# Reordering the first loads, the casts of later inputs and the stores of w1 in a seven-product MLP kernel

## The chip, the cores and the metric

The kernel runs on one core of one Trainium2 chip. The metric is device time of one execution in microseconds (us). In the profile PE is TensorE (matmul), PEld its weight loads, DVE is VectorE, ACT is ScalarE, POOL is GpSimd and SP is SyncE; a `q` after the name (SPq) means the engine's sequencer issuing DMA. PEclk is the share of full clock that the throttle granted to TensorE.

## The reference

```python
# x [8, 1024, 1024], w1 [1024, 4096], w2 [4096, 1024], all float32
h = x @ w1
h = 0.5 * h * (1 + np.tanh(np.sqrt(2 / np.pi) * (h + 0.044715 * h ** 3)))
return (h @ w2).astype(np.float32)
```

## The kernel before

The 8192 tokens go through in eight superblocks of 1024. Each matrix product is split into 2x2 blocks and done with seven block products in place of eight (Strassen's scheme, one level), which takes 448 matmuls of 128x128 by 128x512 for a layer of a superblock. Products 2 and 5 use a raw block of the weight; the other five use a sum or difference of two blocks. These seven "operands" in fp16 are made once, in superblock 0, stored to DRAM (14.7 MB for each weight) and loaded from there in every later superblock. The second layer of superblock 0 is done plainly, with 512 matmuls, while the operands of w2 are being made.

Three parts matter. The first is how superblock 0 makes w1: 512-byte runs of w1 in, a cast on ScalarE, five sums on VectorE, and three stores at once from the POOL queue.

```python
w1v = w1.rearrange("(k p) (b c n) -> b c p k n", p=P, b=2, n=P)    # n = 128 floats = 512 bytes

def make_w1(c):                      # for each of 16 column blocks, in superblock 0
    raw = {}
    for b in range(2):
        st = gcp.tile([P, 2 * KH, P], F32, name="gc")              # 3 buffers
        nc.sync.dma_start(out=st, in_=w1v[b, c])                   # SP queue
        r = rawp.tile([P, 2, KH * P], DT, name="raw")              # 5 buffers
        nc.scalar.copy(out=r..., in_=st...)                        # ACT cast to fp16
        ...
    ops = w_operands([v[:, j] for j in range(5)], raw)             # DVE: five sums
    nc.gpsimd.dma_start(out=w1_d[c][:, 0:5, :], in_=v)             # POOL queue
    for j, m in enumerate(PLAIN):
        nc.gpsimd.dma_start(out=w1_d[c][:, 5 + j, :], in_=ops[m])  # releases raw
    ...
```

The second is how x of a later superblock comes in: eight casting DMAs (fp32 to fp16, DRAM to DRAM) from the POOL queue into rows of 128 elements (256 bytes), then eight transposing DMAs from the SP queue.

```python
def x_later(s):
    xr = x2[s * SB:(s + 1) * SB, :].rearrange("t (k c) -> k t c", c=P)
    xb = xdram.tile([2 * KH, SB, P], DT, name="xb")
    xT = xtp.tile([P, 2 * KH, SB], DT, name="xT")
    for k in range(2 * KH):
        nc.gpsimd.dma_start(out=xb[k], in_=xr[k])
    for k in range(2 * KH):
        nc.sync.dma_start(out=xT[:, k, :], in_=xb[k], transpose=True)
    return xT
```

The third is the loop. The text calls the casts of the next superblock after the first layer of this one. The scheduler that turns the text into instruction streams did not keep that order: in the trace of the kernel before these casts, which have no input but x itself, were issued from 1.3 us on.

```python
xT = x_first()                       # superblock 0: x transposed by PE
for sb in range(NSB):
    xs = x_sums(xT)
    g = matmul1(xs, make_w1 if sb == 0 else load_w1)
    if sb + 1 < NSB:
        xT = x_later(sb + 1)
    (matmul2_first if sb == 0 else matmul2)(sb, g)
```

In `matmul2_first` the fp32 rows of w2 are loaded on the SP queue, cast on ScalarE, used, summed on VectorE and stored from the POOL queue.

Of the kernel before, what the change touches and what calls it, by code (L numbers as in the profile page):

```python
# [8 lines left out]
F32 = mybir.dt.float32  # L9
# [39 lines left out]
PLAIN = (2, 5)  # L49


@with_exitstack
def kernel(
# [21 lines left out]
    WP = 8  # L75

    xtp = ctx.enter_context(tc.tile_pool(name="xtp", bufs=2))
    xsp = ctx.enter_context(tc.tile_pool(name="xsp", bufs=1))
    gp = ctx.enter_context(tc.tile_pool(name="gp", bufs=1))
    gcp = ctx.enter_context(tc.tile_pool(name="gcp", bufs=3))  # L80
    wp = ctx.enter_context(tc.tile_pool(name="wp", bufs=6))
    rawp = ctx.enter_context(tc.tile_pool(name="rawp", bufs=5))
# [6 lines left out]
    w1v = w1.rearrange("(k p) (b c n) -> b c p k n", p=P, b=2, n=P)  # L89
    w2v = w2.rearrange("(a c p) (b o) -> b c p a o", a=2, p=P, b=2)  # L90

    w1_d = [dram.tile([P, 7, KH * P], DT, name=f"w1_d{c}") for c in range(NI)]
    w2_d = [dram.tile([P, 7, WP, OH], DT, name=f"w2_d{h}") for h in range(NI // WP)]
# [7 lines left out]
    def wtile():  # L101
        return wp.tile([P, WP * OH], DT, name="w")
# [3 lines left out]
    def w_operands(sums, raw):  # L106

        ops = {}
        for j, m in enumerate(SUMS):
            u, op, v = B_TERMS[m]  # L110
            nc.vector.tensor_tensor(out=sums[j], in0=raw[u], in1=raw[v], op=op)  # L111
            ops[m] = sums[j]
        for m in PLAIN:
            ops[m] = raw[B_TERMS[m][0]]
        return ops

    def make_w1(c):
        raw = {}
        for b in range(2):
            st = gcp.tile([P, 2 * KH, P], F32, name="gc")  # L120
            nc.sync.dma_start(out=st, in_=w1v[b, c])
            r = rawp.tile([P, 2, KH * P], DT, name="raw")
            nc.scalar.copy(out=r.rearrange("p a f -> p (a f)"), in_=st.rearrange("p k n -> p (k n)"))  # L123
            for a in range(2):
                raw[f"{a + 1}{b + 1}"] = r[:, a]
        t = wtile()
        v = t[:, : 5 * KH * P].rearrange("p (m f) -> p m f", m=5)
        ops = w_operands([v[:, j] for j in range(5)], raw)
        nc.gpsimd.dma_start(out=w1_d[c][:, 0:5, :], in_=v)
        for j, m in enumerate(PLAIN):  # L130
            nc.gpsimd.dma_start(out=w1_d[c][:, 5 + j, :], in_=ops[m])  # L131
        return {m: o.rearrange("p (k n) -> p k n", n=P) for m, o in ops.items()}

    def load_w1(c):
        t = wtile()
        nc.sync.dma_start(out=t[:, : 7 * KH * P], in_=w1_d[c].rearrange("p m f -> p (m f)"))
        v = t[:, : 7 * KH * P].rearrange("p (m k n) -> p m k n", m=7, n=P)
        return {m: v[:, j] for j, m in enumerate(SUMS + PLAIN)}

    def load_w2(m):  # L140
        j = (SUMS + PLAIN).index(m)
        pieces = []
        for h in range(NI // WP):
            t = wtile()
            nc.sync.dma_start(
                out=t, in_=w2_d[h][:, j].rearrange("p c o -> p (c o)")
            )
            pieces.append(t.rearrange("p (c o) -> p c o", o=OH))
        return pieces
# [3 lines left out]
    def x_sums(xT):  # L153
        blocks = {
            f"{a + 1}{k + 1}": xT[:, k * KH:(k + 1) * KH, a * HT:(a + 1) * HT]
            for a in range(2) for k in range(2)
        }
        ops = {3: blocks["11"], 4: blocks["22"]}
        for m in (5, 1, 2, 7, 6):
            u, v = A_TERMS[m]  # L160
            s = xsp.tile([P, KH, HT], DT, name=f"xs{m}")
            nc.vector.tensor_tensor(out=s, in0=blocks[u], in1=blocks[v], op=SUB)
            ops[m] = s
        return ops

    def x_first():
        identity = consts.tile([P, P], F32, name="identity")
        make_identity(nc, identity)
        xT = xtp.tile([P, 2 * KH, SB], DT, name="xT")
        for s in range(SB // P):  # L170
            xn = tp.tile([P, HT], F32, name="tmp")
            xm = tp.tile([P, HT], F32, name="tmp")
            for k, t in enumerate((xn, xm)):
                nc.sync.dma_start(out=t, in_=x2[s * P:(s + 1) * P, k * HT:(k + 1) * HT])
                ps = psum()
                for j in range(KH):
                    nc.tensor.matmul(
                        ps[:, j * P:(j + 1) * P],
                        lhsT=t[:, j * P:(j + 1) * P],
                        rhs=identity,  # L180
                        is_transpose=True,
                        start=(j == 0),
                        stop=(j == KH - 1),
                    )
                eng = nc.vector.tensor_copy if k == 0 else nc.scalar.copy
                eng(  # L186
                    out=xT[:, k * KH:(k + 1) * KH, s * P:(s + 1) * P],
                    in_=ps.rearrange("p (j t) -> p j t", t=P),
                )
        return xT  # L190

    def x_later(s):
        xr = x2[s * SB:(s + 1) * SB, :].rearrange("t (k c) -> k t c", c=P)
        xb = xdram.tile([2 * KH, SB, P], DT, name="xb")
        xT = xtp.tile([P, 2 * KH, SB], DT, name="xT")
        for k in range(2 * KH):
            nc.gpsimd.dma_start(out=xb[k], in_=xr[k])  # L197
        for k in range(2 * KH):
            nc.sync.dma_start(out=xT[:, k, :], in_=xb[k], transpose=True)
        return xT  # L200

    def tt(out, in0, in1, op):
        nc.vector.tensor_tensor(out=out, in0=in0, in1=in1, op=op)  # L203
# [3 lines left out]
    def matmul1(xs, get_w1):  # L207
        g = {b: gp.tile([P, NI, HT], GT, name=f"g{b}") for b in ("11", "12", "21", "22")}

        def product(bank, w, m, first, last):  # L210
            for k in range(KH):
                nc.tensor.matmul(  # L212
                    bank,
                    lhsT=w[m][:, k, :],
                    rhs=xs[m][:, k, :],
                    start=(first and k == 0),
                    stop=(k == KH - 1),
                    skip_group_check=not first,
                )
# [11 lines left out]

        for c in range(NI):
            w = get_w1(c)
# [23 lines left out]
            late = (c, w, qb, s2)  # L257
        finish(*late)
        return g
# [3 lines left out]
    def store(sb, b, q, src):  # L263
        r0 = sb * SB + (int(b[0]) - 1) * HT + q * P
        o0 = (int(b[1]) - 1) * OH
        nc.gpsimd.dma_start(out=out2[r0:r0 + P, o0:o0 + OH], in_=src)  # L266

    def matmul2_first(sb, g):
# [3 lines left out]
        keep = []  # L272
        for b in range(2):
# [3 lines left out]
            def mm(i, c, w):  # L277
                for a in range(2):
# [3 lines left out]
                        rhs=w[:, a, :],  # L282
# [4 lines left out]
            for c in range(NI):  # L287
                st = gcp.tile([P, 2, OH], F32, name="gc")
                nc.sync.dma_start(out=st, in_=w2v[b, c])
                if b == 0:  # L290
                    if c % 4 == 0:
                        keep.append(wtile().rearrange("p (c a o) -> p c a o", a=2, o=OH))
                    w = keep[-1][:, c % 4]
                else:
                    w = rawp.tile([P, 2, OH], DT, name="raw")
                nc.scalar.copy(out=w, in_=st)  # L296
                ready.append(w)
                if c < NI - TAIL:
                    for i in range(2 * NQ):
                        mm(i, c, w)  # L300
                if b == 1:
                    w0 = keep[c // 4][:, c % 4]
                    raw = {"11": w0[:, 0], "21": w0[:, 1], "12": w[:, 0], "22": w[:, 1]}
                    t = wtile()
                    v = t[:, : 5 * OH].rearrange("p (m o) -> p m o", m=5)
                    ops = w_operands([v[:, j] for j in range(5)], raw)
                    d = w2_d[c // WP]
                    nc.gpsimd.dma_start(out=d[:, 0:5, c % WP, :], in_=v)  # L308
                    for j, m in enumerate(PLAIN):
                        nc.gpsimd.dma_start(out=d[:, 5 + j, c % WP, :], in_=ops[m])  # L310
            for i in range(2 * NQ):
# [7 lines left out]
                store(sb, f"{i // NQ + 1}{b + 1}", i % NQ, o)  # L319

    def matmul2(sb, g):
        def product(m, banks, first):
            pieces = load_w2(m)
            u, v = A_TERMS[m]
            for q in range(NQ):
# [8 lines left out]
                for c in range(NI):  # L334
# [3 lines left out]
                        rhs=pieces[c // WP][:, c % WP, :],  # L338
# [30 lines left out]
        for q, ps in product(7, rb, False):  # L369
            c11 = temp()  # L370
            tt(c11, u[q], ps, ADD)
            store(sb, "11", q, c11)

    xT = x_first()
    for sb in range(NSB):
        xs = x_sums(xT)
        g = matmul1(xs, make_w1 if sb == 0 else load_w1)
        if sb + 1 < NSB:
            xT = x_later(sb + 1)
        (matmul2_first if sb == 0 else matmul2)(sb, g)  # L380
# [30 lines left out]
```

## Time and profile before

| | before |
|---|---|
| median of 4 runs | 1723.96 us (1721.97 to 1725.25) |
| first product starts | 25.5 us |
| first layer of superblock 0, 448 matmuls | 222 us, granted clock 0.76 |
| second layer of superblock 0, 512 matmuls | about 111 us |
| each later superblock, 896 matmuls | 193.4 us |

The first fence is the window view of the kernel before, for four stretches: the start, the first layer, the second layer, and superblock 1. The columns are the stretch, its length, the busy time of each engine with the number of its instructions, the granted clock, the mean share of the 16 DMA engines that was in use (the recorded times of packets are added up, and the sum passes 1 here, with 1.16 and 1.33), and the rate.

```profile
core 0: us, PE busy (x) PEld busy (x) DVE busy (x) ACT busy (x) POOL busy (x), PEclk, DMA share, GB/s
0.00:25.50 25.50, 15.18 (x64) 11.04 (x65) 7.55 (x11) 6.72 (x10) 9.06 (x17) 0.87 1.16 248
25.50:247.50 222.00, 126.66 (x454) 50.20 (x454) 85.60 (x167) 87.01 (x124) 66.79 (x105) 0.76 1.33 245
247.50:358.60 111.10, 111.10 (x511) 50.21 (x510) 36.42 (x91) 25.40 (x29) 33.04 (x51) 0.99 0.92 285
358.60:552.00 193.40, 193.21 (x897) 87.50 (x895) 95.94 (x125) 53.85 (x93) 8.68 (x16) 1.00 0.59 193
```

TensorE is busy all of superblock 1, and so it is in the six after that: 896 matmuls at 0.216 us are 193.4 us. That is the floor of these stages. The first layer of superblock 0 has half as many matmuls and needs 222 us in place of 97. In this stretch the DMA share is above 1 while the rate is only 245 GB/s: the DMA engines are busy and yet do not move much.

The next fence is the chain of waits on the page of the kernel before (the work that ended last, followed back to its releasers), by line. After it comes the view of the tile that the casts write.

```profile
DMA xb<-in_x_dram 9%; POOL out_dram L266 4%; DMA w_d_93<-w 1%; DMA out_dram<-tmp 1%; POOL w_d_103 L310 0%; POOL w_d_102 L310 0%; POOL w_d_102 L308 0%; POOL w_d_103 L308 0%; POOL xb L197 0%; POOLq L266 0%; POOL w_d_101 L131 0%; POOL w_d_100 
```

```profile
L197 POOL DMA_DIRECT2D xb<-in_x_dram x56: 751/758/895, 1.3 to 169.7; - x56
```

The casts in this chain are 9% of the span, about 155 us, and all 56 of them, for all seven later superblocks, were issued between 1.3 and 169.7 us, inside superblock 0. Their 57,344 packets (56 casts of 1024 rows) are three quarters of the 76,672 packets of queue q0.

Three more views show what the casts do to others. The first two are the timeline of POOL, with the two stores of raw blocks of the first column block, and a line of the timeline of ACT. Each line of a timeline has the start, the length, the engine, the line of the source, the operation, and in brackets the idle time before it with what ended it.

```profile
33.56 0.58 POOL L131 DMA_DIRECT2D w_d_86<-raw  x1 [3.24 <-DMA xb<-in_x_dram]
...
57.44 0.57 POOL L131 DMA_DIRECT2D w_d_86<-raw  x1 [0.97 <-DMA xb<-in_x_dram]
```

```profile
54.17 1.05 ACT L123 CAST raw<-gc 128x1024 f16<-128x1024 f32 x1 [14.01 <-DMA w_d_86<-raw]
```

A line from the view of the tile that those stores write (times from issue to landing, in us):

```profile
DMA to landing us min/median/max: 4.4/4.5/20.5
```

On POOL, between the first of these stores (33.6 us) and the second (57.4 us) stand nine casts, and POOL paused before all but one of them for an earlier cast. The first store also needed 20.5 us from issue to landing, where 4.5 is the median; it shares its DMA queue with the casts, but that this is the reason is not shown. Until it landed, at about 54.1 us, it held its raw buffer, and the cast on ACT that needed the buffer had waited 14.0 us ("<-DMA w_d_86<-raw"). The next cast on ACT came at 69.7 us, after another 14.0 us.

The third is the timeline of the SP queue. The text `x2` at the end of a line is the number of instructions in it.

```profile
71.17 4.53 SPq L199 DMA_TRANSPOSE xT<-xb  x1
81.90 0.37 SPq L121 DMA_DIRECT2D gc<-in_w_dram  x1
82.33 9.28 SPq L199 DMA_TRANSPOSE xT<-xb  x2
...
92.28 14.65 SPq L199 DMA_TRANSPOSE xT<-xb  x2
...
107.66 9.42 SPq L199 DMA_TRANSPOSE xT<-xb  x1
...
117.80 12.83 SPq L199 DMA_TRANSPOSE xT<-xb  x2
130.72 79.15 SPq L121 DMA_DIRECT2D gc<-in_w_dram  x18
```

Transposes of x for superblock 1 stand in the same queue as the loads of w1 (L121). The queue did one thing at a time: none of its DMA records (346) overlaps the next. Five times between 71 and 131 us the queue stands at transposes: 4.53 + 9.28 + 14.65 + 9.42 + 12.83 = 50.7 us. No load was issued in that time.

### The profile page before, as it was taken

What the parts mean: (1) busy time and instruction counts of PE and PEld (TensorE: products, weight loads), DVE (VectorE), ACT (ScalarE), POOL (GpSimd) and SP (SyncE); (2) the same over time, 40 slices, a digit from 0 to 9 for tenths busy, and PEclk for the clock granted to TensorE, in tenths of its full rate; (3) what the DMA queues carried; (4) which work ended last, traced back from release to release, by engine and by line L of the source; (5) the groups of instructions that cost most, each with busy time, mean ns of one, the idle gap of its engine ahead of it and who ended that gap; (6) DMA issues with size and microseconds to landing.
All of it is one profiled execution on the core that took longest, in us unless ns stands there. A gap on an engine that the chain in (4) does not pass through costs nothing.

```text
span 1723.7 us, 18773 instructions
## 1 busy us (share of the span) xinstructions
PE 1606.4 (93%) x7296; PEld 724.8 (42%) x7296; DVE 801.8 (47%) x1136; ACT 495.8 (29%) x806; POOL 170.2 (10%) x286
## 2 busy tenths in 40 slices
PE   5246789999999999999999999999999999999997
PEld 3012334444444444444444444444444444444443
DVE  4123642445534555345534565345534565355433
ACT  3123661234310441034310441034310441034310
POOL 2333222310011000100011000100011000100011
PEclk8667899999999999999999999999999999999999
DMA  9999999874765447554755447554755444554451
GB/s 234 210 204 224 308 305 245 285 292 158 199 213 180 152 165 210 197 193 153 218 197 179 155 169 205 198 187 153 213 202 186 158 169 154 199 179 155 169 195 49
DMA packets 210425, 336.78 MB, mean 195 GB/s; under 512 B 125600, under 2 KB 158368, under 8 KB 197792
## 3 DMA queue, kind: packets, MB, share of 16 engines
q1 hardware_dynamic: 133664, 257.98, 49.8%
q0 software_dynamic: 76672, 77.61, 18.2%
q8 instruction: 57, 0.93, 0.2%
q14 instruction: 32, 0.26, 0.0%
HBM read 272.63 MB, written 77.59 MB: 203 GB/s over the span
## 4 chain that ended last, share of the span: by engine, by line
issue 82%; DMA 11%; POOL 6%; POOLq 0%
DMA xb<-in_x_dram 9%; POOL out_dram L266 4%; DMA w_d_93<-w 1%; DMA out_dram<-tmp 1%; POOL w_d_103 L310 0%; POOL w_d_102 L310 0%; POOL w_d_102 L308 0%; POOL w_d_103 L308 0%; POOL xb L197 0%; POOLq L266 0%; POOL w_d_101 L131 0%; POOL w_d_100 L131 0%; POOL w_d_99 L131 0%; POOL w_d_98 L131 0%; POOL w_d_97 L131 0%
## 5 line engine op out<-in xcount | busy, mean ns | idle before, releaser
L203 DVE TENSOR_TENSOR tmp<-tmp,ps 128x512 f32<-128x512 f32 x652 | 447.2, 687 | 699.6 <-PE ps L335 332.3
L212 PEld LDWEIGHTS <-w 128*128 128x128 f16 x3456 | 342.0, 99 | 502.3 <-issue 105.8
L335 PE MATMUL ps<-w,gc 128*128 128x512 f16 x2240 | 485.8, 379 | 0.0
L335 PEld LDWEIGHTS <-gc 128*128 128x128 bf16 x2240 | 219.3, 98 | 264.2
L212 PE MATMUL ps<-xT,w 128*128 128x512 f16 x1024 | 267.7, 384 | 0.7 <-ACT xT L186 0.7
L266 POOL DMA_DIRECT2D out_dram<-tmp x128 | 69.5, 543 | 1327.9 <-ACT tmp L355 951.8
L237 ACT COPY tmp<-ps 128x512 f32<-128x512 f32 x128 | 72.9, 569 | 251.6 <-PE ps L212 251.6
L203 DVE TENSOR_TENSOR tmp<-ps,tmp 128x512 f32<-128x512 f32 x128 | 88.4, 690 | 5.0 <-PE ps L212 0.7
L111 DVE TENSOR_TENSOR w<-raw 128x512 f16<-128x512 f16 x96 | 37.8, 420 | 69.2 <-ACT raw L123 69.2
L123 ACT CAST raw<-gc 128x1024 f16<-128x1024 f32 x32 | 33.4, 1043 | 121.0 <-DMA gc<-in_w_dram 62.9
L355 ACT COPY tmp<-ps 128x512 f32<-128x512 f32 x28 | 16.4, 586 | 177.3 <-PE ps L335 177.3
L212 PE MATMUL ps<-xs_246,w 128*128 128x512 f16 x64 | 21.0, 461 | 45.9 <-ACT g_249 L222 45.9
L197 POOL DMA_DIRECT2D xb<-in_x_dram x56 | 42.5, 761 | 80.5 <-DMA xb<-in_x_dram 76.7
L212 PE MATMUL ps<-xs_244,w 128*128 128x512 f16 x64 | 20.3, 448 | 31.9 <-DVE tmp L203 31.9
L361 ACT COPY tmp<-ps 128x512 f32<-128x512 f32 x28 | 16.4, 586 | 80.3 <-PE ps L335 54.0
L349 ACT COPY tmp<-ps 128x512 f32<-128x512 f32 x28 | 16.4, 586 | 74.4 <-PE ps L335 74.4
L212 PE MATMUL ps<-xs_242,raw 128*128 128x512 f16 x64 | 20.3, 449 | 15.4 <-ACT tmp L237 15.4
L212 PEld LDWEIGHTS <-raw 128*128 128x128 f16 x128 | 14.4, 113 | 39.5 <-issue 26.7
L111 DVE TENSOR_TENSOR w<-w,raw 128x512 f16<-128x512 f16 x48 | 18.6, 419 | 18.0 <-ACT raw L296 18.0
L296 ACT CAST raw<-gc 128x1024 f16<-128x1024 f32 x16 | 16.7, 1045 | 34.8 <-PE ps L279 24.5
L279 PE MATMUL ps<-w,g_249 128*128 128x512 f16 x64 | 25.0, 391 | 0.0
L279 PE MATMUL ps<-w,g_248 128*128 128x512 f16 x64 | 24.8, 387 | 0.0
(236 smaller groups left out, 1759.6 us busy)
## 6 DMA issues: line engine op xcount, KB each, us to landing
w<-w_d_102 SPq DMA_DIRECT2D x49, 1024.0 KB, 5.0
w<-w_d_103 SPq DMA_DIRECT2D x49, 1024.0 KB, 7.0
gc<-in_w_dram SPq DMA_DIRECT2D x64, 512.0 KB, 6.8
out_dram<-tmp POOLq DMA_DIRECT2D x128, 256.0 KB, 2.7
xb<-in_x_dram POOLq DMA_DIRECT2D x56, 256.0 KB, 16.1
w<-w_d_86 SPq DMA_DIRECT2D x7, 896.0 KB, 4.5
w<-w_d_87 SPq DMA_DIRECT2D x7, 896.0 KB, 6.1
w<-w_d_88 SPq DMA_DIRECT2D x7, 896.0 KB, 6.3
```

Of the source, the lines that this page charges most:

```text
L111: nc.vector.tensor_tensor(out=sums[j], in0=raw[u], in1=raw[v], op=op)
L123: nc.scalar.copy(out=r.rearrange("p a f -> p (a f)"), in_=st.rearrange("p k n -> p (k n)"))
L197: nc.gpsimd.dma_start(out=xb[k], in_=xr[k])
L203: nc.vector.tensor_tensor(out=out, in0=in0, in1=in1, op=op)
L212: nc.tensor.matmul(bank, lhsT=w[m][:, k, :], rhs=xs[m][:, k, :], start=(first and k == 0), stop=(k == KH - 1), skip_group_check=not first,)
L237: nc.scalar.copy(out=v, in_=pb)
L266: nc.gpsimd.dma_start(out=out2[r0:r0 + P, o0:o0 + OH], in_=src)
L279: nc.tensor.matmul(banks[i], lhsT=g[f"{i // NQ + 1}{a + 1}"][:, c, (i % NQ) * P:(i % NQ + 1) * P], rhs=w[:, a, :], start=(c == 0 and a == ...
L296: nc.scalar.copy(out=w, in_=st)
L335: nc.tensor.matmul(banks[q], lhsT=a[:, c, :], rhs=pieces[c // WP][:, c % WP, :], start=(first and c == 0), stop=(c == NI - 1), skip_group_ ...
L349: nc.scalar.copy(out=v[q], in_=ps)
L355: nc.scalar.copy(out=c21, in_=ps)
```

## The change

The change has several parts: first loads in one strict order with 2 KB runs; raw fp16 w1 to DRAM first, and its sums made and stored one superblock later; one pool of 26 buffers of 4 KB per partition ("units") in place of several pools. One more part is in the diff: the casts of x are 128 whole rows (2 KB of fp16 each) and are ordered behind another instruction, so that they can no longer be pulled to the start. The diff, cut to its core:

```diff
-    w1v = w1.rearrange("(k p) (b c n) -> b c p k n", p=P, b=2, n=P)
+    w1v = w1.rearrange("(k p) (b i) -> b p k i", p=P, b=2)
+    raw_d = [dram.tile([P, 4, KH * QW], DT, name=f"raw_d{q}") for q in range(NI // QC)]
+    up = ctx.enter_context(tc.tile_pool(name="up", bufs=26))
...
+    def load_in_order(out, in_, **kw):
+        return tc.keep_in_program_order(nc.sync.dma_start(out=out, in_=in_, **kw))
...
+    class MadeQuad:                 # a quarter of w1: 4 column blocks, 512 floats = 2 KB runs
+        def load(self):
+            for b, t in self.raw.items():
+                for k in range(0, KH, 2):
+                    cast_in(t[:, k:k + 2, :], w1v[..., self.q * QW:(self.q + 1) * QW],
+                            nc.scalar.copy if k else pool_copy)
+        def sum(self, m, sl=slice(None)):
+            make_sum(self.ops, m, self.raw, KH, QW, sl)
+            if not self.first:      # superblock 1, not 0
+                nc.gpsimd.dma_start(out=w1_d[self.q][:, m - 1, :], in_=flat(self.ops[m]))
+        def keep_raw(self):         # superblock 0: 2.1 MB for a quarter, not 3.7
+            for b, t in self.raw.items():
+                load_in_order(raw_d[self.q][:, BLOCKS.index(b), :], flat(t))
...
-        for k in range(2 * KH):
-            nc.gpsimd.dma_start(out=xb[k], in_=xr[k])
+    def x_cast(s, after):
+        xb = xdram.tile([SB, H], DT, name="xb")
+        with tc.issue_after(after.ins):
+            for q in range(0, SB, P):
+                nc.gpsimd.dma_start(out=xb[q:q + P, :], in_=x2[s * SB + q:s * SB + q + P, :])
+        return xb
...
+        if sb == 0:
+            xb = x_cast(1, pool_last[0])        # behind the last w1 cast on POOL
+            last, blocks = matmul2_first(sb, g, quad.keep_raw, xb)
+            continue
         if sb + 1 < NSB:
-            xT = x_later(sb + 1)
-        (matmul2_first if sb == 0 else matmul2)(sb, g)
+            blocks = x_transpose(x_cast(sb + 1, last), nc.sync.dma_start)
+        last = matmul2(sb, g)                   # last: this superblock's last output store
```

Superblock 1 loads the raw blocks, makes the sums again and stores all seven operands. The transposes for superblock 1 go to the end of the second layer of superblock 0.

## The prediction

> **What bounds it now.** From 358.0 to 1712.3 us TensorE never waits: the window table shows 193.40 us for each of the seven later superblocks (896 matmuls of 0.216 us), all busy. That part is at its floor. The loss lies in the first superblock. Its first product starts at 25.5 us (timeline), and the 448 matmuls of its first layer take 222 us (25.5 to 247.5) where 448 x 0.216 = 97 us would do, at a granted clock of 0.76. Its second layer (512 matmuls, to 358.0) is at its floor of 110.5 us. After the last matmul come 11.5 us.
>
> The 125 us are lost to DMA: from 25.5 to 175 us the share of the 16 engines is 1.47, at only 213 GB/s, and the chain of waits runs from 4.8 to 173 us almost wholly through the x casts. The view of the cast tile shows all 56 casts, for all seven later superblocks, issued between 1.3 and 169.7 us. They write 256-byte rows: 57,344 packets of about 41 ns, over 16 engines some 147 us of engine time (an estimate from the packet records). Beside them run w1 loads in 512-byte packets, stores of finished operands (14.7 MB), and transposes that hold up the w1 loads behind them on the SP queue. [...] without the casts, from 190 to 240 us, the rate is 317 GB/s.
>
> **What the change does.** The casts go behind the last POOL cast, later behind each superblock's last store, in 2 KB rows: out of the first layer. The finished w1 stores move to superblock 1. Left in the first layer: x 4.2 MB, w1 16.8 MB, 6.3 MB of raw stores. A quarter of w1 is 4.2 MB in 2 KB packets (101 ns each here: 13 us) plus a 2.1 MB store in 4 KB packets (160 ns: 5 us), 18 us against 24.2 us of matmul: TensorE should bind. VectorE comes near: per quarter 20 x 0.69 + 5 x 1.22 = 20 us, more in the first.
>
> Start: the x transposes (0.93 us per four) take some 19 us, then w1's first columns; first product about 21.5 us. First layer 97 [...] + 6 (waits for quarter 1 and VectorE) = 106, to 127.5 us. Second layer 110.5, to 238; its sums, stores and transposes fit within. For the boundary and superblock 1 (raw loads 8.4 MB, stores 14.7 MB) I allow 5. Then 7 x 193.4 = 1354 and 11.5: 238 + 5 + 1354 + 11.5 = 1608.
>
> **Predicted: 1608 us**, 8 in 10 between 1592 and 1640. Faster by over 2%: 0.96; within 2%: 0.03; slower: 0.01.
>
> **What would show it.** Right: first product near 21.5 us, second layer from near 128 us, no cast packets in the first 80 us, later superblocks still 193.4 us. Partly wrong: PE waits in the first quarters on VectorE sums or ScalarE/POOL casts; PE waits at superblock 1's start on transposes or on units held by unfinished stores.
>
> **What would make it wrong.** The 26 units are almost all in use (25 in superblock 1): a late store delays the next quarter's load, then TensorE. The strict queue can block on one full buffer. [...] a POOL cast of several us would starve the first quarters. Superblock 1's 33 MB in 97 us is near the most this trace shows (408 GB/s in 10 us). Each costs 10 to 40 us, not the gain.

Two statements on the hardware that no trace of this case shows are cut from this text, and in the sum of the first layer a term of 3 us, for which no trace is named. With the term that sum was 97 + 3 + 6 = 106 us; without it the terms left come to 103. The 1608 us still contain it (1605 without it).

## The result

The kernel after takes 1619.66 us, the median of four runs (1617.7 to 1620.44). The ratio to the kernel before is 0.9394, with a 95% interval of 0.9378 to 0.9411. Ratios here are the mean time of one kernel's fast runs over that of the other's of the same rounds, so they are not quite the ratio of the medians quoted.

The window view of the kernel after, with four stretches that have the same meaning as before:

```profile
0.00:26.70 26.70, 11.14 (x64) 10.15 (x64) 12.90 (x15) 7.62 (x12) 5.14 (x10) 0.82 0.75 245
26.70:139.70 113.00, 101.81 (x449) 44.73 (x450) 76.24 (x109) 74.36 (x113) 22.18 (x25) 0.95 0.91 308
139.70:249.00 109.30, 109.30 (x508) 49.59 (x507) 46.20 (x44) 20.77 (x25) 12.22 (x23) 1.00 1.00 349
249.00:442.60 193.60, 191.97 (x889) 86.73 (x888) 106.20 (x135) 53.91 (x93) 22.82 (x44) 1.00 0.66 225
```

The first layer fell from 222 to 113 us, at a clock of 0.95 in place of 0.76. The second layer and the later superblocks are as they were. The rate in the first layer rose from 245 to 308 GB/s at a lower share. The chain of waits and the view of the cast tile:

```profile
PE ps L267 33%; PE ps L439 30%; PE ps L375 3%; DMA gc<-in_w_dram 2%; DVE u L107 1%; POOL out_dram L355 1%; DMA u<-raw_d_82 1%; SPq L115 1%; DMA u<-raw_d_83 1%; DMA gc<-in_x_dram 1%; ACT u L137 1%; PE ps L225 0%; DMA xb<-in_x_dram 0%; DMA ou
```

```profile
L244 POOL DMA_DIRECT2D xb<-in_x_dram x56: 486/516/652, 88.0 to 1226.5; - x56
```

No cast comes before 88.0 us, and the chain is now mostly matmuls. What TensorE still waits for is small. These are the two longest in the view of PE's waits (what waited and for what; total us, number, longest):

```profile
PE ps L267 <- ACT tmp L324: 8.9, 1, 8.9
PE ps L267 <- DVE u L107: 8.2, 1, 8.2
```

Both lie in the first layer. The one of 8.2 us is at the first product, the one of 8.9 us at 101 us. The timeline shows the first of them:

```profile
19.34 9.13 DVE L107 TENSOR_TENSOR u<-u 128x2048 f16<-128x2048 f16 x10
...
26.73 5.47 PE L267 MATMUL ps<-u 128*128 128x512 f16 x15 [8.23 <-DVE u L107]
```

VectorE does ten operations in a row. The five differences of x come first among them, and the first sum of w1, which the first product needs, comes after. So the first product waited 8.23 us for VectorE. The second wait, from the same timeline:

```profile
106.19 1.04 ACT L137 CAST u<-gc 128x1024 f16<-128x1024 f32 x1 [9.04 <-DMA gc<-in_w_dram]
...
109.11 0.56 ACT L324 COPY tmp<-ps 128x512 f32<-128x512 f32 x1
...
109.73 3.63 PE L267 MATMUL ps<-u 128*128 128x512 f16 x9 [8.90 <-ACT tmp L324]
```

On ACT a cast of w2 stood before the gelu and the copy that TensorE needed. The SP queue issued four loads of w2 from 88.35 us on, this one among them, and the cast could not start before 106.19 us. It waited 9.04 us, and TensorE then 8.90 us for the copy at 109.11. Between 90 and 100 us the loads got only 24 GB/s, beside 152 GB/s written by the eight casts for superblock 1 (issued from 88.0 us) and 113 GB/s of raw stores (packet records). So the moved casts may themselves hold up this load; no run tests it.

The following table is taken from the order of the matmul records in each trace: start of the first product, then the time to the 449th matmul (first layer), to the end of the 512 plain ones (second layer), and through superblock 1. A few records can be missing, so the stages are good to about a microsecond. Superblocks 2 to 7 took 193.4 us each in every run. The ratio is to the kernel before (medians of 1722.8 to 1725.2 us). Kernels are compared only within the same rounds. All outputs are right.

| run | ratio (95%) | median us | first product | first layer | second layer | superblock 1 |
|---|---|---|---|---|---|---|
| before | 1 | 1724.0 | 25.5 | 220.3 | 112.2 | 193.7 |
| after | 0.9394 (0.9378 to 0.9411) | 1619.7 | 26.7 | 112.8 | 110.5 | 195.6 |
| b1_defer_casts | 0.9415 (0.9401 to 0.9429) | 1624.7 | 20.0 | 132.3 | 110.6 | 194.7 |
| b2_wide_casts | 0.9935 (0.9901 to 0.9968) | 1715.3 | 32.7 | 204.7 | 110.5 | 195.3 |
| a1_early_casts | 0.9678 (0.9661 to 0.9694) | 1670.0 | 51.8 | 140.9 | 110.5 | 195.0 |
| a2_store_w1_at_once | 0.9467 (0.9451 to 0.9483) | 1634.4 | 27.5 | 127.0 | 113.6 | 193.4 |
| a4_512B_w1_runs | 0.9458 (0.9442 to 0.9474) | 1628.6 | 25.5 | 122.7 | 110.5 | 196.5 |
| c1_defer_and_spread | 0.9408 (0.9394 to 0.9422) | 1620.2 | 19.0 | 115.8 | 111.8 | 205.5 |
| c2_defer_spread_wide | 0.9475 (0.9461 to 0.9489) | 1632.0 | 18.4 | 124.5 | 110.5 | 204.4 |
| c3_casts_behind_gelu | 0.9448 (0.9435 to 0.9461) | 1629.1 | 18.9 | 109.7 | 129.9 | 203.3 |
| a3_w2_casts_on_pool | 0.9395 (0.9381 to 0.9409) | 1618.5 | 26.3 | 112.5 | 113.1 | 193.8 |
| v1_w2_casts_behind_gelu | 0.9409 (0.9396 to 0.9422) | 1621.7 | 26.6 | 102.0 | 117.4 | 204.0 |
| v2_first_sum_first | 0.9378 (0.9365 to 0.9391) | 1615.9 | 19.3 | 107.9 | 110.5 | 206.0 |
| v3_first_stores_own_queue | 0.9357 (0.9339 to 0.9375) | 1614.4 | 19.8 | 107.5 | 121.5 | 196.5 |

From before to after the stages sum to +1.2 - 107.5 - 1.7 + 1.9 = -106.1 us, and the two profiled executions differ by 107.8 us (spans 1723.7 and 1615.9; the rest is after the last matmul). The timed medians differ by 104.3 us. The profiled execution of the kernel after was the fastest of its four.

### The profile page after: what moved, and what is told of

Same layout as the page of the kernel before. It is cut to its first block, busy times and chain, and to the rows that moved or that the text cites. A ratio compares the mean times of both kernels' runs of the same rounds, so it can differ in the third digit from the quotient of the medians.

```text
span 1615.9 us, 19003 instructions
## 1 busy us (share of the span) xinstructions
PE 1577.7 (98%) x7296; PEld 718.5 (44%) x7296; DVE 819.7 (51%) x1046; ACT 480.5 (30%) x794; POOL 135.0 (8%) x238
## 4 chain that ended last, share of the span: by engine, by line
PE 66%; issue 23%; DMA 5%; DVE 1%; POOL 1%; SPq 1%; ACT 1%; POOLq 0%; DVEq 0%; ACTq 0%
PE ps L267 33%; PE ps L439 30%; PE ps L375 3%; DMA gc<-in_w_dram 2%; DVE u L107 1%; POOL out_dram L355 1%; DMA u<-raw_d_82 1%; SPq L115 1%; DMA u<-raw_d_83 1%; DMA gc<-in_x_dram 1%; ACT u L137 1%; PE ps L225 0%; DMA xb<-in_x_dram 0%; DMA out_dram<-tmp 0%; SPq L152 0%
## 5 line engine op out<-in xcount | busy, mean ns | idle before, releaser
L267 PE MATMUL ps<-u 128*128 128x512 f16 x3584 | 780.3, 380 | 21.0 <-ACT tmp L324 8.9
L267 PEld LDWEIGHTS <-u 128*128 128x128 f16 x3584 | 351.3, 98 | 448.8 <-issue 21.4
L439 PE MATMUL ps<-u,gc 128*128 128x512 f16 x2240 | 485.8, 379 | 0.0
L107 DVE TENSOR_TENSOR u<-u 128x2048 f16<-128x2048 f16 (+2 forms) x110 | 123.2, 1151 | 58.1 <-ACT u L137 24.7
L324 ACT COPY tmp<-ps 128x512 f32<-128x512 f32 x128 | 72.9, 569 | 261.9 <-PE ps L267 261.8
L459 ACT COPY tmp<-ps 128x512 f32<-128x512 f32 x28 | 16.4, 587 | 177.3 <-PE ps L439 177.3
L137 ACT CAST u<-gc 128x1024 f16<-128x1024 f32 (+1 forms) x52 | 50.2, 978 | 46.0 <-DMA gc<-in_w_dram 45.9
L375 PE MATMUL ps<-u,g_220 128*128 128x512 f16 x128 | 48.5, 379 | 0.0
L375 PE MATMUL ps<-u,g_221 128*128 128x512 f16 x128 | 48.5, 379 | 0.0
L375 PE MATMUL ps<-u,g_222 128*128 128x512 f16 x128 | 48.5, 379 | 0.0
L375 PE MATMUL ps<-u,g_223 128*128 128x512 f16 x128 | 48.5, 379 | 0.0
L465 ACT COPY tmp<-ps 128x512 f32<-128x512 f32 x28 | 16.4, 586 | 80.3 <-PE ps L439 80.3
L453 ACT COPY tmp<-ps 128x512 f32<-128x512 f32 x28 | 16.4, 586 | 74.9 <-PE ps L439 74.9
L244 POOL DMA_DIRECT2D xb<-in_x_dram x56 | 27.6, 514 | 14.4 <-DMA out_dram<-tmp 10.4
L118 POOL CAST u<-gc 128x1024 f16<-128x1024 f32 (+1 forms) x20 | 22.6, 1131 | 64.1 <-DMA gc<-in_w_dram 54.5
L419 ACT COPY tmp<-ps 128x512 f32<-128x512 f32 x8 | 4.7, 585 | 64.7 <-PE ps L375 64.7
L375 PEld LDWEIGHTS <-g_221 128*128 128x128 bf16 x128 | 12.5, 98 | 15.1
L375 PEld LDWEIGHTS <-g_223 128*128 128x128 bf16 x128 | 12.5, 98 | 15.1
```

What stands on the lines that cost most here:

```text
L107: nc.vector.tensor_tensor(out=out, in0=in0, in1=in1, op=op)
L118: pool_last[0] = nc.gpsimd.tensor_copy(out=out, in_=in_)
L137: cast(out=dst, in_=st)
L244: nc.gpsimd.dma_start(out=xb[q:q + P, :], in_=x2[s * SB + q:s * SB + q + P, :])
L267: nc.tensor.matmul(bank, lhsT=ops[m][:, k, cs], rhs=xs[m][:, k, :], start=(first and k == 0), stop=(k == KH - 1), skip_group_check=not first,)
L324: nc.scalar.copy(out=v, in_=pb)
```

## The experiments

The theory to test: the early casts of x are what made the first layer slow, and moving them is what gained. The rivals: the wider runs of w1 and the later stores gained, or it was not where the casts stand but their small packets.

### One part alone, on the kernel before

**b1_defer_casts** is the kernel before with only the order changed: each superblock's casts are issued behind the last DMA that comes before them in the text. The casts keep their 256-byte rows, and w1 its 512-byte runs and immediate stores.

```diff
-        for k in range(2 * KH):
-            nc.gpsimd.dma_start(out=xb[k], in_=xr[k])
+        with tc.issue_after(after[0].ins):     # last store of w1 operands, later of outputs
+            for k in range(2 * KH):
+                nc.gpsimd.dma_start(out=xb[k], in_=xr[k])
```

> The kernel before, with one thing changed: the x casts (still 256-byte rows) are issued behind the last store of w1 operands in superblock 0, later behind each superblock's last output store. Theory C (the early casts take the DMA engines from the first layer): the first layer of superblock 0 falls from 222 us to 110 to 130 us; the transposes may now hold up the second layer's w2 loads by up to 25 us; in all 1625 to 1655 us. Rival W (the w1 traffic itself, its 512-byte loads and the 14.7 MB of finished-operand stores, is what starves TensorE): the first layer stays above 180 us, in all over 1685 us.

It ran at 0.9415, 1624.7 us. That is (1 - 0.9415) / (1 - 0.9394) = 97% of the whole gain, from a few lines. Not all of it comes from the first layer. In the profiled executions 5.7 us lie after the last matmul. The last output packets land 3.0 us after it in every run, but the instruction records show that the DRAIN with which GpSimd ends the program took 4.1 us in b1, 9.6 in the kernel before and 8.1 in the kernel after. No run tells why. Up to the end of superblock 1, by the table, b1 has 94.1 of the 106.1 us, or 89%.

The first layer took 132.3 us, and the trace shows why it is not shorter:

```profile
117.10 26.10 SPq L202 DMA_TRANSPOSE xT<-xb  x8
...
145.76 1.23 DVE L164 TENSOR_TENSOR xs<-xT 128x2048 f16<-128x2048 f16 x1 [20.60 <-DMA xT<-xb]
...
148.24 1.86 PE L215 MATMUL ps<-xs,w 128*128 128x512 f16 x4 [21.86 <-DVE tmp L206]
...
148.87 1.05 ACT L299 CAST w<-gc 128x1024 f16<-128x1024 f32 x1 [24.43 <-DMA gc<-in_w_dram]
```

In such a line `<-` names what the instruction waited for. From 117.1 us the SP queue stood 26.1 us at the eight transposes for superblock 1. VectorE's next operation was a difference of x for superblock 1 (xs<-xT), which waited 20.6 us for those transposes; the sums that TensorE needed stood behind it, so TensorE waited 21.9 us. The loads of w2 stand behind the transposes too: a cast of w2 on ACT waited 24.4 us for its load, and started only at 148.87 us, after TensorE had gone on. So two waits ran side by side, and the one on VectorE released TensorE. Without both waits the first layer would be 132.3 - 21.9 = 110.4 us, by an estimate.

**b2_wide_casts** leaves the casts early and widens them: whole rows, as in the kernel after. In the trace the casts are 896 packets of 16 KB in place of 57,344 of 256 bytes.

```diff
-        xb = xdram.tile([2 * KH, SB, P], DT, name="xb")
-            nc.gpsimd.dma_start(out=xb[k], in_=xr[k])
+        xb = xdram.tile([SB, H], DT, name="xb")
+            nc.gpsimd.dma_start(out=xb[q:q + P, :], in_=x2[s * SB + q:s * SB + q + P, :])
```

> The kernel before, with one thing changed: the 56 casts stay as early as they were but write whole 2 KB rows (16 KB packets of 1.23 us in the profile after: 896 packets over 16 engines are 69 us of engine time, against 147 us for the 256-byte packets). Theory C: about half of the casts' cost goes, in all 1645 to 1680 us. Rival W: within 2% of before, over 1700 us.

This expectation missed: it ran at 0.9935, 1715.3 us. By an estimate from the packet records the casts' engine time fell from 57,344 x 41 ns / 16 = 147 us to 896 x 1.35 us (the mean in this run) / 16 = 76 us, yet only 10 us were gained (1725.2 to 1715.3). By the number alone this is what rival W foretold, but b1 left the w1 traffic as it was and gained 100 us, so W isn't the main cause. The SP queue and the waits of ACT show what remained:

```profile
54.05 12.24 SPq L198 DMA_TRANSPOSE xT<-xb  x1
...
71.42 20.55 SPq L198 DMA_TRANSPOSE xT<-xb  x2
...
96.92 17.19 SPq L198 DMA_TRANSPOSE xT<-xb  x1
```

```profile
ACT raw L123 <- DMA gc<-in_w_dram: 95.3, 15, 17.9
```

Transposes still stood in the SP queue for most of 54 to 114 us (57.3 us in all, against 50.7 in the kernel before), in place of loads of w1, and ACT waited 95.3 us for loads of w1 in all. POOL's queue, however, was set free. The views of the tile xb have POOL's wait for earlier casts, in us and number, first in the kernel before, then in b2:

```profile
  DMA xb<-in_x_dram: 76.7, 33
```

```profile
  DMA xb<-in_x_dram: 4.0, 2
```

So half of the engine time and nearly all of POOL's waiting went, and 10 us were gained: as long as the casts are early, something else costs nearly as much. Two candidates are left. The transposes that depend on the casts stand in the SP queue before loads of w1 (57.3 us). And the wide packets may press back the loads beside them, which is a guess from this: TensorE waited 17.5 us for the first loads of x, against 5.5 in the kernel before, and the first product came 7.2 us later. The two were not separated: a kernel with early casts and late transposes was not made from the kernel before.

### One part undone, in the kernel after

**a1_early_casts** takes the ordering away again and leaves all the rest of the change.

```diff
-        with tc.issue_after(after.ins):
+        if True:
```

> The kernel after, with one thing undone: the casts may be issued at once (they keep their 2 KB rows). Theory C: some 69 us of engine time come back into the first 100 to 150 us, where the 16 engines were already 0.91 busy: 1660 to 1690 us. Rival W: the w1 traffic is still the lean one, so under 1635 us.

It ran at 0.9678, 1670.0 us, within what was expected: 50 us slower than the kernel after. The first product came at 51.8 us, and the first layer took 140.9 us. The view of PE's waits names the loads of x:

```profile
PE ps L225 <- DMA gc<-in_x_dram: 28.6, 6, 5.3
```

Between 10 and 40 us the loads of x got 74 to 94 GB/s in each 10 us, beside casts that wrote 157 to 179 (packet records); in the kernel after they had 267 in the first 10 us and 153 in the next. No transpose by DMA was issued before 222.7 us. So here it is the casts' use of the DMA engines, and no transposes in a queue, that cost most of the 25 us at the start (TensorE waited 7.1 us for x in the kernel after). The rest of the change without the ordering gains 3.2%, the ordering without the rest 5.85%, and both 6.1%. They do not add up, because both take load off the same stretch; once the ordering is there, the rest is worth some 5 us, or 12 up to the end of superblock 1 (the closing DRAIN of b1 is shorter).

**a2_store_w1_at_once** stores the finished operands in superblock 0 (14.7 MB, not 8.4 MB of raw blocks, of which 6.3 in the first layer), and superblock 1 loads them.

```diff
-            if not self.first:
+            if sl == slice(None):
                 nc.gpsimd.dma_start(out=w1_d[self.q][:, m - 1, :], in_=flat(self.ops[m]))
         def keep_raw(self):
-            for b, t in self.raw.items():
-                load_in_order(raw_d[self.q][:, BLOCKS.index(b), :], flat(t))
+            self.copy_plain()
-            if sb > 1:
+            if sb > 0:                          # superblock 1 loads w1_d
```

> The kernel after, with one thing undone: superblock 0 stores the seven finished w1 operands (14.7 MB) itself, no fp16 blocks are kept, and superblock 1 loads the operands as the later ones do. Theory C: the first layer then moves 35.7 MB instead of 27.3 MB, at some 320 GB/s 112 us where it took 113 us, so it is lost only in part: 1620 to 1640 us. Rival W: this is a main part of the gain, over 1650 us.

1634.4 us, as expected, 15 us slower. The first layer is 14.2 us longer and the second 3.1; superblock 1 is 2.2 us shorter. Deferring the stores is worth that in this kernel. It is more than the 5 us of the whole rest of the change, so the worth of a part depends on what stands beside it.

**a4_512B_w1_runs** loads quarters 1 to 3 of w1 in runs of 512 bytes. The edit also makes twice as many loads and casts, each half as large.

```diff
-                for k in range(0, KH, 2):
-                        w1v[int(b[1]) - 1, :, k0 + k:k0 + k + 2, self.q * QW:(self.q + 1) * QW],
+                for c in range(QC):
+                        w1v[int(b[1]) - 1, :, k0:k0 + KH, c0:c0 + P],     # 128 floats
```

> The kernel after, with quarters 1 to 3 of w1 loaded in 512-byte runs (256 KB a transfer) in place of 2 KB runs (512 KB). By b1's packets (512 B in 28 ns, 2 KB in 95 ns) the load rate falls from 345 to 293 GB/s, a quarter from 12.2 to 14.3 us, still under 24 us of matmul: theory C expects 1617 to 1632 us. If the 2 KB runs are a main part of the gain (rival W), over 1645 us.

1628.6 us, as expected, 9 us slower, all of it in the first layer (122.7 us). A 2 KB packet took about 95 ns in b1 and a 512-byte packet 28 ns (94.0 and 28.0 ns on average in the kernel after), so by an estimate the same bytes in short runs cost 4 x 28 / 95 = 1.18 times the engine time. The doubled number of loads and casts may have its part in the 9 us; that was not separated.

### Can the simple version be repaired?

**c1_defer_and_spread** is b1 with the eight transposes for superblock 1 put one each behind eight loads of w2, so that they no longer stand in a block before those loads.

```diff
                 load = nc.sync.dma_start(out=st, in_=w2v[b, c])
+                if b == 1 and 4 <= c < 12:
+                    with tc.issue_after(load.ins):
+                        x_transpose(xb, xT, [c - 4])
```

> b1 with one more edit: superblock 1's eight transposes are issued one at a time behind the w2 loads of blocks 4 to 11 of the second half of w2, not all together in front of 27 w2 loads. If the 21.9 us wait of TensorE in b1 comes from the SP queue holding w2 loads behind transposes (and ScalarE behind a w2 cast), it goes: 1598 to 1608 us, under the kernel after. If that wait has another cause (the DMA engines simply full), it stays: 1620 us or more.

This missed: 1620.2 us, equal to the kernel after within the intervals (by the stages it is 6.5 us slower, with a closing DRAIN 4.0 us shorter). The wait of 21.9 us did go, and the first layer fell to 115.8 us. As the transposes come later for VectorE too, c1 doesn't tell its wait for them from ACT's wait for w2. But superblock 1 rose from 194.7 to 205.5 us. Its largest wait:

```profile
257.81 0.69 DVE L211 TENSOR_TENSOR tmp<-tmp,ps 128x512 f32<-128x512 f32 x1 [8.51 <-DMA out_dram<-tmp]
```

TensorE then waited 7.45 us for VectorE, at 258.55 us. VectorE needed a temporary that was still held by an output store ("out_dram<-tmp"). Those stores are issued from the POOL queue, behind the stores of w2 operands.

**c2_defer_spread_wide** adds the wide casts to c1.

```diff
-        xb = xdram.tile([2 * KH, SB, P], DT, name="xb")
+        xb = xdram.tile([SB, H], DT, name="xb")       # and casts of 128 whole rows, as in b2
```

> c1 with the casts in 2 KB rows besides. Once the casts are out of the first layer their row size should be worth little: within 4 us of c1. If the row size mattered by itself, over 5 us faster than c1.

A miss as well: 1632.0 us, 11.8 us slower than c1. Of this, 5.7 us lie in the stages and 5.2 in the closing DRAIN on GpSimd (9.3 us in place of 4.1), which stays unexplained. In the packet records, between 110 and 130 us of the profile's time, the loads of w2 got 92 and then 135 GB/s (for each 10 us), where in c1 they got 180 and 190. The wide casts have packets of 16 KB (1.23 us each in the kernel after), the casts of c1 packets of 256 bytes (41 ns each in the kernel before). From the rates the author guesses that the large packets held back the loads beside them. This was not shown: no run changes the packet size alone at a fixed place. If it is so, the wide casts of c2 did harm by standing beside urgent loads, and a1 has the same picture at its start; in the kernel after the casts of superblock 1 are wide too, and begin at 88 us.

**c3_casts_behind_gelu** adds to c1 that all casts of w2 in superblock 0 are issued behind the last gelu, so that ACT does not stop in the first layer.

```diff
+                with tc.issue_after(last_gelu[0].ins):
-                nc.scalar.copy(out=w, in_=st)
+                    nc.scalar.copy(out=w, in_=st)
```

> c1 with all w2 casts of ScalarE issued behind the last gelu of superblock 0's first layer. c1's waits of some 8 us at 113 to 135 us stand at gelus behind w2 casts; they should go, at the price of 1 to 3 us where the second layer starts. The 7.5 us wait at 251 us (temporaries held by late output stores) stays. 1610 to 1617 us, so no worse than the kernel after, with its w1 traffic untouched. If over 1622 us, ScalarE's order was not what cost c1.

A miss: 1629.1 us. The first layer fell to 109.7 us, and the second rose to 129.9, with a wait of 16.0 us between 186 and 202 us, and another of 7.0 us at 263 us in superblock 1. In the wait of 16.0 us VectorE stood at sums of w2 that waited for their stores (4.9 and 7.0 us) and at a difference of x that waited for its transpose (3.5 us), with the copies that TensorE needed behind them.

### Can the waits left in the kernel after be taken away?

**a3_w2_casts_on_pool** gives the first half of the w2 casts to POOL, so that they cannot hold up ACT.

```diff
-                            nc.scalar.copy,
+                            nc.scalar.copy if b else nc.gpsimd.tensor_copy,
```

> The kernel after, with the casts of the first half of w2 on POOL, not on ScalarE. If the 8.9 us wait of TensorE at 100.8 us is ScalarE's in-order queue standing at a w2 cast whose load has not landed, with copies and gelus behind it, the wait goes and the time falls by 7 to 11 us, to 1608 to 1613 us. If TensorE there waits for something else (VectorE or DMA alone), no change: 1617 to 1622 us.

A miss: 1618.5 us, no change. The wait at 101 us is gone, and one of the same length is there at 129 us, at the next cast of w2 that ACT still has:

```profile
137.22 1.04 ACT L137 CAST u<-gc 128x1024 f16<-128x1024 f32 x1 [10.39 <-DMA gc<-in_w_dram]
138.18 0.59 ACT L277 ACTIVATE g<-ps 128x512 bf16<-128x512 f32 x1
138.82 1.86 PE L267 MATMUL ps<-u 128*128 128x512 f16 x4 [10.03 <-ACT g L277]
```

The chain is the same as before: ACT waited 10.39 us for a load of w2, and the gelu that TensorE needed stood behind that cast. TensorE waited 8.9 us in the kernel after and 10.0 us here. A cast of 128x1024 took 1.04 us on POOL (L137, all but two of those from 106 us on), as it did on ACT.

**v1_w2_casts_behind_gelu** also issues the second half of those casts behind the last gelu.

```diff
-                            nc.scalar.copy if b else nc.gpsimd.tensor_copy,
+                            late_copy if b else nc.gpsimd.tensor_copy,      # behind the last gelu
```

> a3 with one more edit: the casts of the second half of w2 stay on ScalarE but are issued behind the last gelu of superblock 0's first layer. In a3 ScalarE stood 10.4 us at such a cast (it came up at 126.8 us, its load landed at 137.2 us) with a gelu behind it, and TensorE waited 10.0 us. If ScalarE's program order is the cause of that wait and of the 8.9 us in the kernel after, both go: 1606 to 1611 us. If TensorE is held by the w2 data itself, it will wait as long under another name: 1616 to 1620 us.

The first layer took 102.0 us, 10.8 less than in the kernel after, so the waits of ACT were read correctly. Yet the whole took 1621.7 us. The second layer (117.4) and superblock 1 (204.0) took back all of it. The largest new wait, on VectorE:

```profile
258.03 1.47 DVE L107 TENSOR_TENSOR tmp<-tmp,ps 128x512 f32<-128x512 f32 x2 [9.32 <-DMA out_dram<-tmp]
```

**v2_first_sum_first** adds another order of VectorE's first operations: the first sum of w1 before the differences of x, and the others in the order in which TensorE needs them.

```diff
+            last = self.sum(4, cs)
+            for f, m in ((x_next, 5), (self.sum, 1), (x_next, 1), (x_next, 2), (self.sum, 3),
+                         (x_next, 7), (self.sum, 7), (x_next, 6), (self.sum, 6)):
+                with tc.issue_after(last.ins):
+                    last = f(m, cs) if f == self.sum else f(m)
```

> v1 with VectorE's order at the start changed: the first w1 sum, which the first product needs, goes before the five x differences, and each of the others comes just before its product; the sums of w1's next columns come after the first product's VectorE work. TensorE waits 8.2 us before its first product for that sum in the kernel after. If that wait is VectorE's order alone and w1 then arrives in time, 5 to 8 us faster than v1. If the arrival of w1's next columns (512-byte and 1 KB runs through four buffers, 156 GB/s from 30 to 40 us) bounds the first quarter, TensorE waits there in its place: within 3 us of v1.

(The 156 GB/s are counted from the first packet record, 10.3 us before the profile's zero; by the window view 30 to 40 us has 233 GB/s, and 20 to 30 us has 153.) This was right: the first product came at 19.3 us, in place of 26.6, and the time is 1615.9 us, 5.8 less than v1. The wait of VectorE on output stores is still there, 11.94 us at 252 us.

**v3_first_stores_own_queue** issues the 16 output stores of superblock 0 from ACT's queue, away from POOL's. It also moves the cast of superblock 2's x, which had stood behind the last of these stores (left out of the cut).

```diff
-        return nc.gpsimd.dma_start(out=out2[r0:r0 + P, o0:o0 + OH], in_=src)
+        return (nc.gpsimd if sb else nc.scalar).dma_start(out=out2[r0:r0 + P, o0:o0 + OH], in_=src)
```

> v2 with superblock 0's sixteen output stores issued from ScalarE's DMA queue in place of POOL's, where the last eight stand among superblock 1's w1 stores (and the cast of superblock 2's x ordered behind the last plain w1 store in place of the last output store). In v2 TensorE waits 10.9 us at 242 us: VectorE has no free temporary, for the last of them are held by output stores not yet landed. If the POOL queue's order is the cause, that wait goes: 1603 to 1609 us, the fastest so far. If the DMA engines are simply full there (419 GB/s), TensorE waits as long for the stores or for the next quarter: 1613 to 1617 us.

The wait on output stores did go: superblock 1 fell from 206.0 to 196.5 us. The second layer rose from 110.5 to 121.5 us, with this as its largest wait:

```profile
193.43 0.59 ACT L441 COPY tmp<-ps 128x512 f32<-128x512 f32 x1 [5.30 <-DMA u<-xb]
194.07 2.29 PE L397 MATMUL ps<-u,g 128*128 128x512 f16 x5 [4.87 <-ACT tmp L441]
```

1614.4 us is the best time, 0.4% under the kernel after: the intervals (0.9339 to 0.9375, and 0.9378 to 0.9411) just do not overlap. It was run at another time. The expectation of 1603 to 1609 was missed, and the rival that the wait would come back elsewhere was right.

### Where the removed waits go

Summed over first product, first layer, second layer and superblock 1, the runs on the kernel after give: after 445.6, a3 445.7, v1 450.0, v2 443.7, v3 445.3 us. By an estimate TensorE alone would need about 20 (the first product of v2) + 97 + 110.5 + 193.4 (448, 512 and 896 matmuls of 0.216 us) = 421 us. So 25 us remain, they move from place to place, and taking one away does not shorten the sum. The windows of 150 to 200 and of 200 to 265 us offer a reason. First the kernel after, then v3:

```profile
150.00:200.00 50.00, 50.00 (x234) 22.67 (x232) 18.93 (x18) 11.75 (x13) 4.36 (x8) 1.00 1.00 314
200.00:265.00 65.00, 63.38 (x294) 28.50 (x293) 27.59 (x29) 7.57 (x14) 17.23 (x33) 1.00 1.02 384
```

```profile
150.00:200.00 50.00, 42.47 (x182) 18.09 (x181) 16.47 (x17) 10.70 (x12) 0.00 (x0) 0.93 0.97 272
200.00:265.00 65.00, 62.37 (x289) 28.16 (x288) 27.96 (x29) 7.94 (x14) 9.06 (x17) 1.00 0.99 382
```

In v2, not shown, the shares were 1.02 and 1.02. In all three the DMA share is about 1 in both windows, so on average the DMA engines are near full from 150 to 265 us. By 265 us the kernels had moved nearly the same: 85.2 MB (after), 85.1 (v1), 86.2 (v2) and 84.7 (v3). If the engines were full, a first layer that ends earlier would not make these bytes arrive earlier, and TensorE would wait for them later. This fits all four runs, but it is argued from shares and sums, and narrower windows speak against it in part. These are 180 to 190 us, in the kernel after and in v3:

```profile
180.00:190.00 10.00, 10.00 (x48) 4.51 (x46) 6.01 (x6) 1.99 (x4) 1.66 (x3) 1.00 0.72 151
```

```profile
180.00:190.00 10.00, 6.53 (x27) 2.38 (x26) 6.79 (x8) 1.76 (x3) 0.00 (x0) 1.00 0.55 141
```

Here the DMA engines have room (in v2 the share is 0.97). It is where the 16 transposes for superblock 1 stand as one block in the SP queue (from 170.2 us for 27.4 us in the kernel after, from 168.7 us for 31.0 us in v3), and v3's wait of 5.30 us above is put down to one of them. So the fault of the kernel before, transposes in front of other transfers in one queue, is still there in a smaller form. The 16 transposes (2.1 MB, 256-byte pieces of 2 KB rows) went at about 77 GB/s in the kernel after. In the kernel before, eight that read contiguous 256-byte rows (2.1 MB too) took 21.7 us, about 97 GB/s, in superblock 0, and 14.4 us, about 146 GB/s, at best later. They ran beside other transfers, with 253, 259 and 241 GB/s over the whole core, so the rate of one alone was not measured. Neither a run that takes bytes out of this stretch nor one that spreads these transposes was made; the cause of the 25 us stays open.

## Why the prediction was right

The measured 1619.66 us is within the predicted 1592 to 1640 and 11.7 us above the 1608 named. Point by point:

- **What bounds it and where.** Right: almost only the first layer of superblock 0 changed (220.3 to 112.8 us). The later superblocks are still at 193.4 us, and the second layer took 110.5 us as predicted.
- **The casts move out of the first layer.** Right: no cast came before 88.0 us. b1 shows that this alone gives 97% of the gain in time, and 89% of it up to the end of superblock 1.
- **Why the casts cost.** Half right. The prediction put engine time of 256-byte packets first (147 us) and gave the transposes in the SP queue one clause. a1 shows that the casts' use of the DMA engines is a cost by itself (most of 25 us at the start, with no transposes in the way). But b2 took away about half of the engine time of the packets and nearly all of POOL's waiting for casts, and gained only 10 us. What the transposes in the SP queue and the engines' time are worth against each other stays open.
- **First product.** Mis-sized: 21.5 us predicted, 26.7 measured (+5.2). The order of VectorE's operations was not costed; v2 brought it to 19.3 us.
- **First layer.** Mis-sized: 106 predicted, 112.8 measured (+6.8). The prediction allowed 6 us of waits for the first quarters; the trace has 8.9 us from a w2 cast in ACT's stream, which it did not foresee. The term of 3 us was for a lower clock at the start, and some 2 us are there by an estimate: the granted clock was 0.58 in the first 5 us of the layer and 1.00 in the next 5. TensorE was busy 101.8 of the 113.0 us.
- **Boundary and superblock 1.** The allowance of 5 us was more than enough: superblock 1 took 195.6 us, 2.2 over its floor. Here the prediction was too slow.
- **POOL casts starving the first quarters.** It did not happen: PE's waits name POOL nowhere. A POOL cast of 1024 elements took 1.04 us at best and 1.19 on average; the longest, 1.97 us at 86.1 us, ran beside sums of VectorE, but it held nothing up. That one slowed the other was not shown.
- **The profiled sum.** 5.2 + 6.8 - 2.8 - 1.7 (9.8 us after the last matmul, not 11.5) = +7.5 us. The prediction's terms sum to 1608.5, and this gives the profiled span of 1615.9 us within 0.1. The time of that execution is 1.8 us more than its span, and as it was the fastest of four, the median is another 2.0 us above it. The errors partly cancel, which is luck.

## What to carry to other kernels

Look first at where a transfer without inputs is issued: here the scheduler put the prefetches for the whole program (56 casts, by 169.7 us) in front of the work that starts it, and one ordering constraint was worth more than a rewrite of the layout (100 us in b1, 10 us in b2). The early transfers cost in DMA time (a1: most of 25 us at the start), and their transposes took the SP queue in place of loads (50.7 us in the kernel before); in b1 VectorE, which computes with their result, waited 20.6 us for them. So read the queues of the issuing engines and not just the share of the DMA engines. When waits are taken away one by one and the sum of the stages stays the same, look at the whole stretch before you move the next wait, and in narrow windows, since a mean share near 1 hid 10 us here in which the DMA engines had room (0.72 in the kernel after, 0.55 in v3).
